# Values and output gates of a gated linear attention layer as seven half-size products through DRAM

## The chip, the core and the metric

The kernel runs on one NeuronCore of a Trainium2 chip. The metric is the device time of one execution in microseconds, median of the runs. Names of engines: PE is TensorE (matmul; PEld its weight loads), DVE VectorE, ACT ScalarE, POOL GpSimd, SP SyncE, whose queue issues the DMAs. Every engine executes its own instructions in the order in which the program holds them.

## The reference

A decoder trunk of two layers on x of 1 x 1024 x 1024 (sequence S, width D), all float32. Layer 0 mixes tokens with a dilated sliding-window attention, layer 1 with gated linear attention (GLA); each mixer is followed by an MLP with squared ReLU, each sub-layer has a norm ahead and a residual add behind. The change concerns the GLA mixer:

```python
proj = h @ w_in                       # 1024 -> 512 q, 512 k, 1024 v, 1024 g_out, 16 gate_lr
gk = gate_lr @ w_gate_up + b_gate
log_a = log_sigmoid(gk) / 16          # per head (4), chunks of 64 tokens
b = cumsum(log_a, axis=chunk)
q_t, k_t = q * DK**-0.5 * exp(b), k * exp(-b)
A = where(causal, q_t @ k_t.T, 0)
U = (k * exp(b_last - b)).T @ v       # per chunk; the state S runs over the chunks
o = A @ v + q_t @ S_prev              # 256 values per head
o = rmsnorm(o, norm_w) * silu(g_out)
out = o @ w_out
```

## The kernel before

**Arithmetic.** A float32 operand is cut in two parts of type fp32r: hi, rounded by ACT, and lo, the rest, subtracted on DVE (or POOL). A product is three matmuls: hi x hi, hi x lo, lo x hi (`mm3`, L212 to L215). Matmuls are 128 x 128 by 128 x 512; a block of 128 x 512 results over K = 1024 has 24 of them, in one of eight PSUM banks (`bank`).

**Seven products.** Larger products are cut into halves in each dimension and made as seven products of half size in place of eight, with sums of operands on DVE ahead (`sum1` to `sum4` on the left, differences of weights on the right) and sums of results behind. Class `Values` does this for the values of layer 0: 14 steps for each of three weight matrices, step n being half m of product q (`place`). In a step, `sums` copies finished accumulators out of PSUM (ACT) or adds them to such a copy (DVE), `prep(n + 2)` makes the two parts `dh` and `dl` of the weights of the step after next, `load(n + 5)` asks for weights, `product(n)` issues 24 matmuls. The accumulators are two sets of four banks, A and B, used in turns. `Halves` norms, transposes (`turn`) and cuts (`cut`) the left operand. The MLP (`Up`, `Down`) works in the same way.

**Order.** The program's order is written by hand (manual schedule); tiles come from pools: h8 (12 tiles of 8 KB a partition), k4 (25 of 4 KB), t2 (8 of 2 KB), and an instruction that needs a new tile waits until its last user is done. Work beside the matmuls is cut into steps: `tick()`, called twice per block, runs what `later(n, fn)` has set for that tick, then one entry of `steps`, then `W.pump()`, which loads and splits the next weights of class `Weights`; one of two is split on DVE, the other with `W.second` (POOL by default).

**From the MLP of layer 0 into GLA.** The last steps of `Down` are n = 52 and 53 and then `run_end` with four blocks t = 0 to 3. `first_rows` at n = 46 and 49 norms the first half of the rows; `norm_T` at n = 53 and in `run_end` transposes them into `hT` (eight h8 tiles, hi and lo); `norm_after` does the second half a few ticks later.

**GLA.** Heads go in two pairs. For pair 0: `values` (L292) makes V, 8 blocks of 128 tokens by 512, copied by ACT at L295; then the low-rank product for `lrT` (L1846, L1849) over both halves of the tokens; `start_gates(0)`; `gla_out_gates` (L1727) makes the output gates G, 8 blocks, each with the chain

```python
            act.activation(d, ps, AF.Exp, scale=-1.0)
            dve.tensor_scalar(d, d, 1.0, 3e38, op0=OP.add, op1=OP.min)
            act.activation(e, d, AF.Ln)
            act.activation(e, e, AF.Exp, scale=-1.0)
            dve.tensor_tensor(d, d, e, op=OP.mult)
            dve.scalar_tensor_tensor(e, d, 2.0, e, op0=OP.subtract, op1=OP.mult)
            dve.scalar_tensor_tensor(e, ps, -1.0, e, op0=OP.mult, op1=OP.mult)
```

(L1734 to L1740) and a multiplication by the norm weight on POOL (L1741). Then `gla_keys(h)` (L1799) makes queries and keys of a head: four times half a product (`dense_T`), with `gates` (L1747: bias product pg, Abs, Exp, Ln on ACT, a scan on DVE, subtractions on POOL) started half a head ahead. `gla_unit(h)` (L1648) puts the head's attention into `steps`: `a_step` (scores, masked into AM at L1658), `u_step` (state), `o_step` (output, norm factor `rstd_of`, gate). So the unit of head h runs in the ticks of later products: head 0's in the keys of head 1, head 1's in those of head 2 and the first blocks of the second `values`, head 2's in the keys of head 3, head 3's in the output projection. Order of the products: V pair 0, low rank, G pair 0, keys 0, 1, 2, V pair 1, G pair 1, keys 3.

Of the kernel before, what the change touches and what calls it, by code (L numbers as in the profile page):

```python
# [9 lines left out]
F32 = mybir.dt.float32  # L10
# [4 lines left out]
OP = mybir.AluOpType  # L15
# [26 lines left out]
def hybrid_trunk(ctx, tc, x, norm_mix, norm_mlp, norm_fin, a_in, a_out, g_in, g_up, g_b, g_nw,  # L42
# [68 lines left out]
    class Weights:  # L111
        def __init__(self):
            self.slots = []
            self.ndma = 0
            self.nprep = 0
            self.used = 0
            self.freed = 0
            self.limit = 5
            self.second = pool
            self.parts = {}  # L120
            self.raws = {}

        def add(self, src):
            self.slots.append(src)

# [8 lines left out]
        def prep(self, eng=pool):  # L134
# [12 lines left out]
            act.activation(hi, src, AF.Copy)  # L147
            eng.tensor_tensor(lo, src, hi.bitcast(F32), op=OP.subtract)  # L148
# [26 lines left out]
    def add_wide(w, c0):  # L175
        for j in range(4):
            W.add(cols(w, c0, 512, 2 * j, 2))

# [4 lines left out]
    def add_rows(w, k0):  # L183
        for k in range(2):
            W.add(w[P * (k0 + k):P * (k0 + k + 1), :])
# [3 lines left out]
    def plan_gla():  # L189
        for pair in range(2):  # L190
            if pair == 1:
                add_two(g_in, 512 + DK * 2, DK * 2)
            add_wide(g_in, 1024 + 512 * pair)
            if pair == 0:
                W.add(cols(g_in, 3072, RANK))
            add_wide(g_in, 2048 + 512 * pair)
            for h in ((0, 1), (3,))[pair]:
                add_two(g_in, 512 + DK * h, DK * h)
        for k in range(0, KT, 2):
            add_rows(g_out, k)  # L200
# [45 lines left out]
    def new_hT():  # L246
        return ([h8([P, 2, S], F32R, "hTh") for _ in range(4)],
                [h8([P, 2, S], F32R, "hTl") for _ in range(4)])

# [16 lines left out]
    def norm_T(xn, pair, hT):  # L266
        for kp in range(4):
            norm_T1(xn, pair, kp, hT)

    def norm_T1(xn, pair, kp, hT):  # L270
        transpose_pair(lambda k, i: xn[i][:, 256 * kp + 128 * k:256 * kp + 128 * k + 128],
                       hT[0][kp][:, :, 256 * pair:256 * pair + 256],
                       hT[1][kp][:, :, 256 * pair:256 * pair + 256])

    def mov(hT, kt, half):
        return tuple(t[kt // 2][:, kt % 2, 512 * half:512 * half + 512] for t in hT)

    def stat(hT, kt, lo, step=1):
        return tuple(t[kt // 2][:, kt % 2, lo:lo + (P - 1) * step + 1:step] for t in hT)

    def dense_T(w, hT, half, done):

        ps = bank("pd")
        for kt in range(KT):
            a, b = mov(hT, kt, half)
# [6 lines left out]
    def values(blocks):  # L292
        w = W.take(4)
        V = [h8([P, 4, 512], F32, "V") for _ in range(2)]
        dense_wide(w, hT, blocks, lambda n, ps: act.activation(V[n // 4][:, n % 4, :], ps, AF.Copy), True)  # L295
        return V

    def dense_wide(w, hT, blocks, done, last=False):
        for n, (lo, step) in enumerate(blocks):
            ps = bank("pd")  # L300
            for kt in range(KT):
                a, b = stat(hT, kt, lo, step)
                wh, wl = w[kt // 2]
                mm3(ps, a, b, wh[:, kt % 2, :], wl[:, kt % 2, :], kt == 0, kt == KT - 1)
                if last and n == len(blocks) - 1 and kt % 2:
                    W.free(1)
                if kt == 3:
                    tick()
            done(n, ps)
            tick()  # L310
# [27 lines left out]
    class Halves:  # L338

        def __init__(self, xs, wbc, up, spill=True):  # L340
# [10 lines left out]
        def norm(self, p, step=512):  # L351
            self.xn[p] = norm_scale([self.xs[p][:, 0, :], self.xs[p][:, 1, :]], self.wbc, step, self.y.pop(p, None))
            if self.spill:
                sp.dma_start(xmid[256 * p:256 * p + 256, :].rearrange("(i p) d -> p i d", p=P), self.xs[p])
# [29 lines left out]
        def cut(self, name, c):  # L384
# [4 lines left out]
                   "s3": a.get((1, 0)), "s4": a.get((0, 1))}[name]  # L389
            self.split(name, src, c, self.one, self.two if name in ("s2", "s3", "s4") else self.one)  # L390

        def sum3(self):
            a = self.a
            for c in range(2):
                self.combine(c, a[1, 0], a[0, 0], a[1, 0], OP.subtract)
# [49 lines left out]
        def finish(self):  # L445
# [40 lines left out]
            split("s3", a[1, 0], self.two)  # L486
# [248 lines left out]
    vscr = drp.tile([S, NG, AW], F32, name="vscr")  # L735

    class Values:

        STEPS = 14 * NG
        BLOCKS = ((1, 0), (0, 0), (0, 1), (1, 1), (1, 1), None, (1, 0))  # L740
# [9 lines left out]
        def load(self, n):  # L750
# [10 lines left out]
            sp.dma_start(t, cols(a_in, g * 3 * AW + 2 * AW + 512 * c, 512, 4 * k + 2 * m, 2))  # L761
# [57 lines left out]
        def copy(self, name, s, t):  # L819
# [9 lines left out]
        def add(self, name, s, t, g):  # L829
# [3 lines left out]
            row = 512 * half + 128 * t  # L833
            sp.dma_start(vscr[row:row + 128, g, 512 * quad:512 * quad + 512], c)

        def sums(self, n):
# [5 lines left out]
            for t in (2 * m, 2 * m + 1):  # L842
                if q == 1:
                    self.copy("c11", "B", t)
                elif q == 2:
                    self.add("c11", "A", t, g)
                elif q == 3:
                    self.copy("c22", "B", t)
                elif q == 4:
                    self.copy("c12", "A", t)  # L850
                elif q == 5:
                    self.add("c12", "B", t, g)
                elif q == 6:
                    self.copy("c21", "A", t)
                    self.add("c22", "A", t, g)

        def step(self, n):
# [3 lines left out]
            self.product(n)  # L861

# [347 lines left out]
    hs = Halves(x0, wbc, vals, False)  # L1210
# [163 lines left out]
    def out_proj(layer, wbc_row, o, up):  # L1374
# [5 lines left out]
        W.second = pool if layer else dve  # L1380
# [30 lines left out]
        W.second = pool  # L1411
# [3 lines left out]
        st = Halves(xs, wbc, up)  # L1415
# [14 lines left out]
    class Down:  # L1430
# [117 lines left out]
        def store_rows(self, p):  # L1548
            sp.dma_start(self.spill[256 * p:256 * p + 256, :].rearrange("(i p) d -> p i d", p=P), self.xs[p])

        def first_rows(self, p):
            self.xn = getattr(self, "xn", {})
            self.xn[p] = norm_scale([self.rows(2 * p), self.rows(2 * p + 1)], self.wbc)
            self.store_rows(p)

        def hook(self, n):
            if n == 40:
                self.wbc = load_norm_w(self.next_norm)
            if self.spill is not None:
                if n in (46, 49):  # L1560
                    self.first_rows(n // 49)
                elif n == 53:
                    plan_gla()
                    self.hT = new_hT()
                    norm_T(self.xn.pop(0), 0, self.hT)
# [6 lines left out]
            elif n >= 52:  # L1572
                for t in (2 * (n - 52), 2 * (n - 52) + 1):
                    self.fin[t] = (sm([P, 2], "ss"), k4([P, D], F32, "fin"))
                    self.half_out(t, 1)

# [8 lines left out]
        def run_end(self):  # L1585

            for t in range(4):
                if t == 1 and self.spill is not None:
                    norm_T(self.xn.pop(1), 1, self.hT)
# [3 lines left out]
                if self.spill is not None:  # L1593
                    if t % 2:
                        norm_after(self.xs, 2 + t // 2, self.wbc, self.hT, 4 + t // 2, self.spill)
                    tick()
# [17 lines left out]
    def norm_after(xs, pair, wbc, hT, lag, spill):  # L1614
        xn = norm_scale([xs[pair][:, 0, :], xs[pair][:, 1, :]], wbc)
        sp.dma_start(spill[256 * pair:256 * pair + 256, :].rearrange("(i p) d -> p i d", p=P), xs[pair])
        later(lag, lambda: norm_T(xn, pair, hT))

    def mlp(i, up, next_norm, spill):
# [5 lines left out]
        return d.hT if spill is not None else None  # L1625
# [3 lines left out]
    hT = mlp(0, up, norm_mix[1], xscr)  # L1629


    gc = r6([P, 1412], "gc")
# [283 lines left out]
```

## Time and profile before

| | |
|---|---|
| median of 3 runs | 2700.9 us (2699.88 to 2704.93) |
| the profiled execution's own time | 2703.08 us |
| its span, first to last instruction | 2701.3 us, mean granted clock 0.991 |
| busy PE / DVE / ACT / POOL | 2642.5 / 1788.8 / 1239.4 / 92.2 us |
| POOL instructions | 72 |
| DMA | 402.16 MB, mean 149 GB/s |

How to read profile rows: in a timeline, start and duration in us, engine, line, operation, result<-operands, shape, count, and in brackets the engine's idle time before it with what ended it. In windows, each stretch with its length, busy time of the engines with the number of instructions, the granted TensorE clock (1.00 is full) and DMA. Matmuls overlap in the pipeline: their pace is read from start to start, not from their durations.

### The profile page before, as it was taken

The numbers are of one execution on the slowest core, as the hardware profiler recorded it, in microseconds if no ns is written. First come the engines' busy times: TensorE is split into PE (matmuls) and PEld (weight loads), VectorE is DVE, ScalarE is ACT, GpSimd is POOL, SyncE is SP. The second block draws the span as 40 slices with busy tenths as digits, with TensorE's granted clock in tenths as the row PEclk, the third lists the DMA queues.
The fourth block names the chain that finished last, engine by engine and source line by source line (L and its number), as shares of the span: only waits on it lengthen the run. The fifth ranks groups of instructions, "written<-read, shape, count | busy, mean of one in ns | idle before, by whom it ended". The sixth has DMA issues, their size and how long they took to land.

```text
span 2701.3 us, 33223 instructions
## 1 busy us (share of the span) xinstructions
PE 2642.5 (98%) x12248; PEld 2184.9 (81%) x12248; DVE 1788.8 (66%) x2944; ACT 1239.4 (46%) x2300; POOL 92.2 (3%) x72
## 2 busy tenths in 40 slices
PE   7999999999999899999999999999999999999998
PEld 5888888888888787888888887778888788888887
DVE  7645788888888668666656672562557766656567
ACT  6332455555555345545533343432425555453343
POOL 0000000000000000000000001321200000000000
PEclk9999999999999999999999999999999999999999
DMA  4543455665657533444765453012223444486543
GB/s 152 171 149 113 106 155 137 155 156 140 157 145 206 170 117 123 158 166 138 288 234 187 144 170 113 24 36 66 74 98 114 148 163 139 151 315 217 189 148 125
DMA packets 311411, 402.16 MB, mean 149 GB/s; under 512 B 18864, under 2 KB 183216, under 8 KB 311248
## 3 DMA queue, kind: packets, MB, share of 16 engines
q1 hardware_dynamic: 311248, 400.04, 46.7%
q8 instruction: 96, 1.57, 0.2%
q14 instruction: 67, 0.55, 0.1%
HBM read 267.13 MB, written 107.68 MB: 139 GB/s over the span
## 4 chain that ended last, share of the span: by engine, by line
PE 59%; DVE 5%; ACT 2%; issue 1%; DVEq 0%; ACTq 0%
PE pB L1503 13%; PE pA L1503 10%; PE pX L629 8%; PE pd L213 5%; PE pd L215 5%; PE pd L214 5%; PE pV L629 5%; PE pZ L629 2%; PE pY L629 2%; PE pT L263 1%; PE pO L1678 1%; PE pU L1664 0%; PE pO L1677 0%; PE pT L366 0%; DVE wbl L567 0%
## 5 line engine op out<-in xcount | busy, mean ns | idle before, releaser
L1503 PE MATMUL pB<-dh 128*128 128x512 f32 x512 | 199.4, 389 | 0.0
L1503 PE MATMUL pB<-dh,dl 128*128 128x512 f32 x512 | 199.2, 389 | 0.0
L1503 PE MATMUL pB<-dl,dh 128*128 128x512 f32 x512 | 199.2, 389 | 0.0
L222 DVE TENSOR_TENSOR dl<-sin,dh 128x1024 fp32r<-128x1024 f32 x112 | 136.6, 1220 | 42.9 <-ACT dh L219 42.3
L629 PE MATMUL pV<-s4h,wd 128*128 128x512 f32 x448 | 153.6, 405 | 6.3 <-DVE rb L654 6.3
L219 ACT ACTIVATE dh<-sin 128x1024 fp32r<-128x1024 f32 x112 | 117.8, 1052 | 88.4 <-PE pB L1503 35.5
L924 ACT ACTIVATE pt<-pt,orow 128x128 f32<-128x128 f32 (+1 forms) x192 | 85.0, 444 | 148.0 <-DVE orow L922 143.5
L219 ACT ACTIVATE dh<-kept 128x1024 fp32r<-128x1024 f32 x64 | 67.9, 1061 | 183.3 <-DVE kept L1468 136.5
L1503 PE MATMUL pA<-dh 128*128 128x512 f32 x384 | 149.4, 389 | 0.0
L1503 PE MATMUL pA<-dl,dh 128*128 128x512 f32 x384 | 149.4, 389 | 0.0
L1503 PE MATMUL pA<-dh,dl 128*128 128x512 f32 x384 | 149.4, 389 | 0.0
L567 DVE TENSOR_TENSOR wbl<-t,wbh 128x1024 fp32r<-128x1024 f32 x56 | 68.6, 1225 | 73.6 <-ACT wbh L566 73.6
L1503 PEld LDWEIGHTS pB<-dh,dl 128*128 128x128 f32 x512 | 96.1, 188 | 20.0
L1503 PEld LDWEIGHTS pB<-dl,dh 128*128 128x128 f32 x512 | 96.1, 188 | 19.9
L1503 PEld LDWEIGHTS pB<-dh 128*128 128x128 f32 x512 | 96.1, 188 | 19.8
L567 DVE TENSOR_TENSOR wal<-raw,wah 128x512 fp32r<-128x512 f32 x112 | 76.2, 687 | 47.7 <-ACT wah L566 47.7
L629 PEld LDWEIGHTS pV<-s4h,wd 128*128 128x128 f32 x448 | 85.7, 191 | 25.8 <-DVE rb L654 8.0
L638 ACT ACTIVATE c<-c 128x512 f32<-128x512 f32 x64 | 40.4, 632 | 134.6 <-DVE c L666 83.2
L213 PE MATMUL pd<-whi,hTh 128*128 128x512 f32 x256 | 100.5, 393 | 0.0
L148 POOL TENSOR_TENSOR wlo<-raw,whi 128x1024 fp32r<-128x1024 f32 x16 | 40.0, 2499 | 1765.9 <-ACT whi L147 1762.9
L215 PE MATMUL pd<-whi,hTl 128*128 128x512 f32 x256 | 99.7, 389 | 0.0
L214 PE MATMUL pd<-wlo,hTh 128*128 128x512 f32 x256 | 99.6, 389 | 0.0
(307 smaller groups left out, 7458.0 us busy)
## 6 DMA issues: line engine op xcount, KB each, us to landing
sin<-acts SPq DMA_DIRECT2D x112, 512.0 KB, 3.7
raw<-in_mlp_w_up_dram SPq DMA_DIRECT2D x64, 512.0 KB, 5.7
acts<-s SPq DMA_DIRECT2D x64, 512.0 KB, 3.4
raw<-in_mlp_w_down_dram SPq DMA_DIRECT2D x64, 512.0 KB, 4.6
raw<-in_attn_w_in_dram SPq DMA_DIRECT2D x96, 256.0 KB, 4.4
cw<-c SPq DMA_DIRECT2D x192, 128.0 KB, 2.3
acts<-c SPq DMA_DIRECT2D x64, 256.0 KB, 2.1
kept<-in_mlp_w_down_dram SPq DMA_DIRECT2D x32, 512.0 KB, 5.0
```

What stands on the lines that cost most here:

```text
L148: eng.tensor_tensor(lo, src, hi.bitcast(F32), op=OP.subtract)
L213: pe.matmul(ps, sh, mh, start=start, stop=False)
L214: pe.matmul(ps, sh, ml, start=False, stop=False)
L215: pe.matmul(ps, sl, mh, start=False, stop=stop)
L219: act.activation(hi, src, AF.Copy)
L222: dve.tensor_tensor(lo, src, hi.bitcast(F32), op=OP.subtract)
L263: pe.transpose(ps[:, k, 128 * i:128 * i + 128], src(k, i), ident)
L567: self.remain(lambda: dve.tensor_tensor(lo, src, hi.bitcast(F32), op=OP.subtract))
L629: pe.matmul(st[b], u[:, k, :], v, start=first and k + n == 0, stop=k == 3 and n == 2, skip_group_check=True)
L638: act.activation(r, r, AF.Relu)
L924: act.activation(pt[:, i, :128 * n], pt[:, i, :128 * n], AF.Exp, scale=-1.0, bias=m, accum_out=self.row[:, r, HD:HD + 1])
L1503: pe.matmul(self.acc[s][t], a[:, k, c], b[:, k, :], start=fresh and m + k + v == 0, stop=m == 7 and k == 1 and v == 2, skip_group_check=True)
```

## The change

Values and output gates of all four heads are made first, as 2 x 14 steps of a new class `Mixed(Values)`: first the gates (g = 0, weight columns from 2048), then the values (g = 1, from 1024). Results go to DRAM (`ggscr`, `gvscr`), from where `load_head` reads 1 MB each of V and G per head, three ticks into that head's keys. The four quarters of the gates stay in h8 tiles (`gq`); `gate()`, called after each product from step 7 on, closes one piece (128 x 512) and opens the next, one piece per step. The left operand is cut by `Halves` for seven products; a11, a12, a22 and a21 (cut in steps 20 and 21) then serve as `hT` for the keys. `between` spreads the norms and cuts over `run_end`; `turn(0)` and `turn(1)` stand in steps 52 and 53.

The order afterwards is: gates, values, low rank, keys 0, 1, 2, 3, and each head's unit runs in the keys of the next. `start_gates(0)` follows the first half of the low-rank product. Outputs are treated in pairs of blocks (one bank, one `rstd_of` for two). The norm weight of GLA is multiplied into the rows of the output weights (`add_rows(..., by)`). All work of POOL in GLA (subtractions in `gates`, one of the q_s products, second weight splits) goes to DVE; POOL keeps memsets.

```diff
+    class Mixed(Values):
+        STEPS = 28
+        def source(self, g):
+            return g_in, (2048, 1024)[g]
+        def copy(self, name, s, t, g):
+            if g:
+                return super().copy(name, s, t, g)
+            if t == 0:
+                self.quad[name] = h8([P, 4, 512], F32, "gq")
+            c = self.c[name, t] = self.quad[name][:, t, :]
+            act.activation(c, self.acc[s][t], AF.Copy)
+        def made(self, c, g, rows, cols):
+            if g:
+                sp.dma_start(gvscr[rows, cols], c)
+            else:
+                self.todo.append((c, rows, cols))
+        def gate(self):
+            if self.open is not None:
+                c, rows, cols, d, e = self.open
+                dve.tensor_tensor(d, d, e, op=OP.mult)
+                dve.scalar_tensor_tensor(e, d, 2.0, e, op0=OP.subtract, op1=OP.mult)
+                dve.scalar_tensor_tensor(c, c, -1.0, e, op0=OP.mult, op1=OP.mult)
+                sp.dma_start(ggscr[rows, cols], c)
+                self.open = None
+            if self.todo:
...
+                act.activation(d, c, AF.Exp, scale=-1.0)
+                dve.tensor_scalar(d, d, 1.0, 3e38, op0=OP.add, op1=OP.min)
+                act.activation(e, d, AF.Ln)
+                act.activation(e, e, AF.Exp, scale=-1.0)
+                self.open = c, rows, cols, d, e
...
+    def gla_values():
+        hs, m = down.hs, down.mixed
+        m.product(0)
+        hs.turn(2)
+        m.prep(3)
+        m.load(4)
+        m.product(1, [0, 1])
+        hs.turn(3)
+        m.product(1, [2, 3])
...
+        for n in range(4, m.STEPS):
+            m.sums(n)
+            if n == 4:
+                hs.cut("s2", 1)
+            m.prep(n + 2)
+            m.load(n + (4 if n < 5 else 5))
+            if n == 4:
+                m.load(9)
+            m.product(n)
+            if n == 4:
+                hs.sum4()
+                hs.cut("s4", 0)
+            elif n == 5:
+                hs.cut("s4", 1)
+                hs.sum3()
+                hs.cut("s3", 0)
+            elif n == 6:
+                hs.cut("s3", 1)
+                hs.cut("a22", 0)
+            elif n == 7:
+                hs.cut("a22", 1)
+            if n >= 7:
+                m.gate()
+            if n == 22:
+                plan_gla()
+                W.limit = 3
+            if n in (20, 21):
+                hs.cut("a21", n - 20)
+            if n >= 24:
+                W.pump()
+        for t in range(4):
+            m.add("c21", "B", t, 1)
...
+        def between(self, t):
+            hs, mixed = self.hs, self.mixed
+            if t == 0:
+                mixed.rounded(0)
+                hs.cut("a12", 0)
+                mixed.remain(0)
+            elif t == 1:
+                hs.rstd(2)
+                hs.cut("a12", 1)
+                mixed.prep(1)
+            elif t == 2:
+                hs.norm(2)
+                hs.cut("a11", 0)
+            else:
+                hs.rstd(3)
+                hs.cut("a11", 1)
+                hs.norm(3)
+                mixed.prep(2)
...
-            pool.tensor_tensor(m, m, a, op=OP.subtract)
+            dve.tensor_tensor(m, m, a, op=OP.subtract)
...
-    V = values(nat)
+    hT = gla_values()
     W.take(1)
...
         act.activation(lrT[:2 * RANK, 512 * half:512 * half + 512], ps[:2 * RANK, :], AF.Copy)
+        if half == 0:
+            start_gates(0)
         tick()
     W.free(1)
-    start_gates(0)
-    G = gla_out_gates()
     W.limit = 4
-    for h in range(2):
-        gla_unit(h, V, G, *gla_keys(h))
-    keys = gla_keys(2)
...
+    for h in range(GH):
+        rows = []
+        later(3, lambda: rows.extend((load_head(gvscr, h, "V"), load_head(ggscr, h, "gG"))))
+        got = gla_keys(h)
+        gla_unit(h, *rows, *got)
```

More of the change, by code (lines that the diff above doesn't have):

```diff
@@ L290, in dense_T @@
         tick()
[L292 to L310, printed above, removed]
     class Split:
@@ L843, in sums @@
                 if q == 1:
-                    self.copy("c11", "B", t)
+                    self.copy("c11", "B", t, g)
                 elif q == 2:
@@ L1559, in hook @@
             if self.spill is not None:
[L1560 to L1565, printed above, removed]
+                if n == 46:
+                    self.mixed = Mixed()
+                    self.hs = Halves(self.xs, self.wbc, self.mixed, self.spill)
+                    self.hs.norm(0)
+                elif n == 49:
+                    self.hs.norm(1)
+                elif n >= 52:
+                    self.hs.turn(n - 52)
+                    for k in range(2):
+                        self.mixed.load(2 * (n - 52) + k)
             elif 44 <= n < 48:
@@ L1844, in hybrid_trunk @@
         for kt in range(KT):
-            for n, t in enumerate(mov(hT, kt, half)):
+            for n, t in enumerate(hT[half][kt // 4].parts(kt % 4)):
                 pe.matmul(ps[:2 * RANK, :], W.both[:, kt, :], t, start=kt + n == 0, stop=kt + n == KT)
```

225 lines of the change are left out of this document (105 added, 120 removed).

## The prediction

> **What bounds the kernel now.** I read the page first: the share of each engine and the chain of work that ended last.
>
> ```profile
> PE 2642.5 (98%) x12248; PEld 2184.9 (81%) x12248; DVE 1788.8 (66%) x2944; ACT 1239.4 (46%) x2300; POOL 92.2 (3%) x72
> ...
> PE 59%; DVE 5%; ACT 2%; issue 1%; DVEq 0%; ACTq 0%
> ```
>
> PE is busy 98% of the span and holds the chain, so a matmul that goes is worth its full time wherever PE waits for nobody. Next I cut the stage that changes into stretches: the first values product, the keys of head 0, the keys of head 2, and the second values and gates.
>
> ```profile
> 1623.80:1671.10 47.30, 47.30 (x227) 39.53 (x226) 12.89 (x24) 12.59 (x23) 2.62 (x2) 1.00 0.35 107
> 1723.30:1752.50 29.20, 27.15 (x110) 20.33 (x109) 16.18 (x24) 12.42 (x25) 14.48 (x11) 0.94 0.05 20
> 1788.30:1826.00 37.70, 35.85 (x157) 28.40 (x157) 23.63 (x69) 16.22 (x51) 8.61 (x9) 0.95 0.15 50
> 1826.00:1916.80 90.80, 90.80 (x402) 74.99 (x400) 30.54 (x62) 29.02 (x52) 16.23 (x11) 1.00 0.18 60
> ```
>
> Columns: stretch, length, then busy time of PE, PEld, DVE, ACT and POOL, granted clock, DMA. In the dense products (first and last row) PE is never idle and the clock is 1.00, while DVE works a third of the time or less. PE loses time only in the keys: 2.05 us idle in one stretch, 1.85 us in the other, each with a lower clock.
>
> ```profile
> 1660.30 0.60 ACT L295 ACTIVATE V<-pd 128x512 f32<-128x512 f32 x1 [4.84 <-PE pd L215]
> ```
>
> ACT copies a finished block and then waits 4.84 us for PE: one block of 24 matmuls takes 0.60 + 4.84 = 5.44 us, 0.227 us a matmul. Values and output gates of both halves are 32 blocks, 174.1 us.
>
> **What goes: matmuls.** Seven products of half size for each of the two matrices are 28 steps of 24 matmuls, 672 for 768: 96 x 0.227 = 21.8 us less PE work, all of it on the path. Other matmuls and transposes keep their number.
>
> **What goes: GpSimd's stalls.**
>
> ```profile
> 1734.84 0.66 PE L1821 MATMUL pk<-ident,kdT 128*128 128x128 f32 x4 [2.05 <-DVE kdT L1816]
> ...
> 1736.01 0.63 PE L215 MATMUL pd<-hTh,wlo 128*128 128x512 f32 x1
> 1736.43 0.63 PE L213 MATMUL pd<-hTh,whi 128*128 128x512 f32 x1
> ...
> 1732.06 2.39 DVE L1815 TENSOR_TENSOR kdT<-k_m,dec 128x256 f32<-128x256 f32 x1
> 1734.38 0.41 DVE L1816 TENSOR_TENSOR kdT<-pd,es 128x256 f32<-128x256 f32 x1
> ```
>
> PE waited 2.05 us for kdT because DVE's L1815, running beside a GpSimd instruction, took 2.39 us where the next one of the same size took 0.41 us. Afterwards matmuls start every 0.42 us, not 0.227: half clock. With a clock of 0.94 over 29.2 us that costs 1.75 us more, and 0.95 over 37.7 us costs 1.9 us in the other stretch. With GpSimd silent both stalls should go: 2.05 + 1.75 + 1.85 + 1.9 = 7.6 us. If DVE's longer queue keeps either, the bound is 0.
>
> On the half clock the Trainium skill speaks otherwise (TensorE: Matmul & The Clock Gate, HAM oscillation — how this bites in real kernels): it puts the limit for idle gaps at about 3.4 us. Here a gap of about 2 us was enough, so I price stalls with the half clock; by the page's rule the two half-clock terms that I add further down, 3.3 us, would fall away.
>
> **What is added: the gates' chain.** In the order of the changed program's instructions, step n (n from 7) holds on DVE: sums of finished quarters, the weight's difference (in 8 of 14 steps), the low part dl for step n+2, the three closing operations of the gate before, and the opening one (TS) of this gate. On ACT: copies of finished quarters, dh for step n+2, then Exp, Ln, Exp of this gate. Both run in order, so this is a ring: Ln waits for TS; the next step's copies and dh wait behind Ln and Exp; dl waits for dh; the three closings and the next TS wait behind dl. Its links, from the gates of before and the values of layer 0:
>
> ```profile
> 1685.94 0.43 DVE L1735 TENSOR_SCALAR gd<-gd 128x512 f32<-128x512 f32 x1 [4.84 <-ACT gd L1734]
> 1687.73 0.69 DVE L1738 TENSOR_TENSOR gd<-gd,ge 128x512 f32<-128x512 f32 x1 [1.36 <-ACT ge L1737]
> 1688.46 0.69 DVE L1739 SCALAR_TENSOR_TENSOR ge<-gd,ge 128x512 f32<-128x512 f32 x1
> 1689.19 0.69 DVE L1740 SCALAR_TENSOR_TENSOR ge<-pd,ge 128x512 f32<-128x512 f32 x1
> 1689.80 1.21 DVE L1769 TENSOR_TENSOR_SCAN ga<-gc,gmn 128x512 f32<-128x512 f32 x1
> ...
> 1686.41 0.63 ACT L1736 ACTIVATE ge<-gd 128x512 f32<-128x512 f32 x1 [0.49 <-DVE gd L1735]
> 1687.07 0.63 ACT L1737 ACTIVATE ge<-ge 128x512 f32<-128x512 f32 x1
> ...
> 67.42 1.07 ACT L826 ACTIVATE c<-pB 128x512 f32<-128x512 f32 x2
> 68.38 1.06 ACT L795 ACTIVATE dh<-raw 128x1024 fp32r<-128x1024 f32 x1
> ...
> 80.42 1.06 ACT L795 ACTIVATE dh<-kept 128x1024 fp32r<-128x1024 f32 x1 [1.35 <-DVE kept L771]
> ...
> 79.17 1.22 DVE L771 TENSOR_TENSOR kept<-kept 128x1024 f32<-128x1024 f32 x1
> 81.51 1.22 DVE L801 TENSOR_TENSOR dl<-kept,dh 128x1024 fp32r<-128x1024 f32 x1 [1.13 <-ACT dh L795]
> 82.66 1.22 DVE L771 TENSOR_TENSOR kept<-kept 128x1024 f32<-128x1024 f32 x1
> ```
>
> From start to start: TS to Ln 0.47, Ln to Exp 0.66, Exp 0.63, two copies 0.96 (67.42 to 68.38), dh to dl 1.09 (80.42 to 81.51), dl 1.15, three closings 2.07 (1687.73 to 1689.80). A step with copies takes 7.03 us round the ring. With a difference and two sums instead (0.43 + 1.15, two sums priced as one 1024-wide operation, difference to dh 1.25) it is 7.14 us; without either 6.07, and 6.2 with four sums. In steps 20 and 21 ACT also rounds a21, 1.0 us more for the next ring. Gates are open from step 7 to 22. The 15 rings between come to 7 x 7.03 + 2 x 8.03 + 4 x 7.14 + 6.2 + 6.07 = 106.1 us, where PE's 15 steps need 81.6. DVE's own work there, 15 x (1.15 + 2.07 + 0.43) + 19 x 1.15 for differences, sums and a21 = 77 us, would fit; the order does not let it.
>
> PE cannot run ahead of the ring: product n (even) writes its third block into a bank that step n-1 must first have copied or summed, so of two steps' lead it keeps little. The next late thing after the ring starts is therefore always a bank.
>
> **Where the ring starts.** The second turn now stands before run_end's products, so these run unbroken up to 1623.8, the same moment as before; the first of their four blocks ends at 1623.8 - 3 x 2.72 = 1615.6 and DVE can add it at 1616.1. From there DVE has no pause worth the name.
>
> ```profile
> 1619.80 1.06 ACT L243 ACTIVATE junk<-xs 128x1024 bf16<-128x1024 f32 x1 [2.10 <-DVE xs L1509]
> ...
> 1623.09 2.74 DVE L256 SCALAR_TENSOR_TENSOR xn<-xs,y,wbc 128x512 f32<-128x512 f32 x4
> ```
>
> A norm's factor takes 3.3 us from its second Square to the scaling (1619.80 to 1623.09), the scaling 2.74. During run_end DVE has four adds (half of 1.15 each, 2.3), four low parts of a12 and a11 (4.6), three dl (3.45), two factors (6.6) and two scalings (5.5): 22.5, to 1638.6. Then 23 operations or pairs of 1.15 (one dl, sums 1 to 4, parts of s1, s2, s4, s3 and a22, two sums of quarters, two dl: 26.5), four weight differences with their dl at 82.66 - 79.17 = 3.49 (14.0), and waits for ACT at s1 and the last dl, estimated at 2.5 from the 1.13 us wait above: 43.0, to 1681.6, the first TS. On the way PE waits some 2.5 us for xn of the last rows, as DVE is at 1636 with them where PE wants them at 1634; it costs nothing more, for the ring decides later.
>
> **The end of the stage.** The last TS is at 1681.6 + 106.1 = 1787.7. PE's product 24 gets its third bank 2.3 us later (Ln, Exp and one copy), does 18 matmuls (4.1) and three steps (16.3), and pays about 1.5 for half clock: 1811.9. The quarter c21 finds no free buffer until the store of c11 has landed: 0.6. So 1812.5 - 1623.8 = 188.7 us. Before, the same work took 174.1 plus two turns of 1.8 (47.3 less 8 x 5.44 = 3.8 for both): 177.9. The stage gets longer by 10.8 us although 21.8 us of matmuls are gone.
>
> **The low-rank product.** It used to be followed by 8 blocks of gates; now its bias product pg comes straight after each half.
>
> ```profile
> 1678.58 0.59 ACT L1849 ACTIVATE lrT<-pd 32x512 f32<-32x512 f32 x1 [3.12 <-PE pd L1846]
> 1679.63 0.69 ACT L1762 ACTIVATE ga<-pg,gc 128x512 f32<-128x512 f32 x1 [0.46 <-PE pg L1761]
> ...
> 1691.04 0.73 ACT L1757 ACTIVATE eb<-ga 128x256 f32<-128x256 f32 x2 [3.34 <-DVE ga L1769]
> ```
>
> The first pg waits for its copy, 0.59 and two hand-overs, 1.0 us. The second waits for a copy that stands on ACT behind three Exp of half 0, which wait for DVE's scan: pg to Abs 0.7, three functions 2.0, subtraction 0.7 (now on DVE), scan 1.2, Exp 1.1, copy 0.6 make 6.3 from the first pg, where 16 matmuls take 3.6: 2.5 us, and 1.8 at half clock after it. Together 5.3 us; the bounds are 1.0 (no half clock, copy early) and 7.
>
> **Hidden or nothing.** Heads read values and gates back in 1 MB loads, asked for three ticks into one head and needed in the next.
>
> ```profile
> ol<-oscr SPq DMA_DIRECT2D x2, 1024.0 KB, 9.7
> ```
>
> A load of that size landed in 9.7 us; the shortest time to its first use, in head 0, is four more half blocks and a tick, over 15 us. If two loads shared the rate, about 4 us would show, once. DVE in the heads gets GpSimd's subtractions, the q_s product and half of the weight parts, but only four normalising chains instead of eight: nothing, at worst the rival below. W.second changes nothing in layer 0, where the trace has no POOL work.
>
> **Sum.** +10.8 + 5.3 - 7.6 = +8.5 on a span of 2701.3: 2709.8. The profiled execution took 2703.08, its span lies 0.4 above the median of the runs, 2700.9; on the median I say 2709.
>
> **The rivals.**
> 1. PE keeps the stage: the ring does not hold it, because the lead of two steps or faster hand-overs hide it. Then 28 steps at 5.44, no half clock but for 4.3 us at the late rows: -21.8 - 7.6 + 5.3 + 4.3 = -19.8, 2681. For it: DVE's 77 us of work in 81.6, and PE at 47.30 of 47.30 in the old stage. Against it: the links above, each in order. It decides when a ring is under 5.44 us. Chance 0.13.
> 2. The ring is there but shorter, say 6.2 us each, as some links overlap: 13 us less, 2696. Chance 0.12.
> 3. DVE becomes the bound in the heads too: with GpSimd's five operations in its order and waits for Ln, a half head takes more than PE's 17 us (half of 37.7 less the 3.7 lost); 1.5 us for each of six halves, 2718. Against it: in 1788.30:1826.00 DVE was busy 23.63 of 37.70. Chance 0.08.
> 4. Buffers: SP, in order, waits for a free k4 tile before a load, and stores queue behind it; 8 us more, 2717. Chance 0.07.
>
> My forecast has 0.60, with its own range of 2701 to 2717 (5.3 and 7.6 between their bounds, 3 us on the start). All rivals but the first lie within 2690 to 2721, which leaves out about 0.17. A measurement of this kernel tells 0.2%, 5.4 us, from no change. Faster by more: rival 1 and a third of rival 2, 0.17. Within: the rest of rival 2 and the lower part of my own range, 0.25. Slower: 0.58.
>
> **What would show it.** In the changed profile: PE waits at every second product of the new stage for a copy or sum on ACT or DVE, some 1 to 3 us each; successive TS about 7 us apart; granted clock under 1.00 there; no POOL work and no 2 us wait at kdT; a wait of about 2.5 us at the second pg. Wrong would be: steps of 5.44 us between the gates, PE full in the new stage, or its loss elsewhere, in the heads or behind a load.

## The result and the profile after

The changed kernel takes 2721.7 us, median of four runs (2714.8 to 2722.0), where the kernel before took 2700.7 on the same chip: a ratio of 1.0068, 95% interval 1.0049 to 1.0088. It is slower, as forecast, by more than forecast: 2709 was said, and 2721.7 lies 0.7 us above the end of the range. The profiled execution took 2722.04 us with a span of 2719.9, 18.6 more than the span before.

The page of the changed kernel, engines and chain:

```profile
PE 2633.1 (97%) x12152; PEld 2168.6 (80%) x12152; DVE 1864.6 (69%) x2995; ACT 1269.5 (47%) x2320; POOL 1.8 (0%) x7
...
PE 53%; DVE 8%; ACT 4%; issue 2%; DMA 1%; SPq 0%; DVEq 0%; ACTq 0%
```

96 matmuls are gone (12152 for 12248), but PE's busy time fell by only 9.4 us instead of 21.8, in part because more of the rest runs at the lower clock (0.989 in the mean for 0.991), and the chain now goes through DVE (8% for 5%) and ACT (4% for 2%). The stretches show where (length, busy time of PE, PEld, DVE, ACT and POOL, granted clock, DMA): from the transposition of the last rows to the low-rank product; then the first keys; then heads 0, 1 and 2, each from its score block to that of the next head.

```profile
1632.30:1811.80 179.50, 158.35 (x652) 125.78 (x653) 134.24 (x177) 87.55 (x134) 0.95 (x1) 0.95 0.37 113
...
1824.20:1853.90 29.70, 29.70 (x121) 22.76 (x121) 17.05 (x32) 12.62 (x25) 0.00 (x0) 0.94 0.18 63
1853.90:1897.20 43.30, 40.75 (x170) 31.15 (x170) 25.76 (x67) 15.64 (x47) 0.00 (x0) 0.92 0.20 68
1897.20:1938.80 41.60, 39.03 (x169) 30.47 (x168) 25.03 (x65) 15.64 (x47) 0.00 (x0) 0.96 0.31 102
1938.80:1979.50 40.70, 37.08 (x182) 30.45 (x181) 24.39 (x57) 14.05 (x39) 0.00 (x0) 1.00 0.49 159
```

The new stage keeps PE idle for 21 us at a clock of 0.95, where the dense products before had neither. The heads lose time too, 2.6, 2.6 and 3.6 us of idle PE and clocks of 0.92 and 0.96 in the first two; that part the forecast did not have.

The new stage first. The opening operation (TS) of the gates on DVE, first two and last two of 16:

```profile
1678.45 0.42 DVE L872 TENSOR_SCALAR gd<-gd 128x512 f32<-128x512 f32 x1
1685.36 0.42 DVE L872 TENSOR_SCALAR gd<-gd 128x512 f32<-128x512 f32 x1
...
1775.65 0.42 DVE L872 TENSOR_SCALAR gd<-gd 128x512 f32<-128x512 f32 x1
1785.13 0.42 DVE L872 TENSOR_SCALAR gd<-gd 128x512 f32<-128x512 f32 x1
```

Fifteen rings (from one TS to the next) take 1785.13 - 1678.45 = 106.7 us, where 106.1 was forecast; the first is 6.91 us long, the last 9.48. PE's waits in that stretch and at the bias product after it, from PE's timeline:

```profile
1687.64 0.50 PE L783 MATMUL pA<-dh,s3h 128*128 128x512 f32 x1 [1.72 <-ACT gq L850]
...
1717.10 0.80 PE L783 MATMUL pB<-dh,a12h 128*128 128x512 f32 x1 [3.49 <-DVE gq L798]
...
1771.04 0.80 PE L783 MATMUL pB<-dh,s4h 128*128 128x512 f32 x1 [3.71 <-ACT c L793]
...
1787.41 0.50 PE L783 MATMUL pA<-dh,s3h 128*128 128x512 f32 x1 [2.77 <-ACT c L793]
...
1816.37 1.12 PE L1827 MATMUL pg<-lrT,gc 32*128 32x512 f32 x2 [0.68 <-ACT lrT L1917]
...
1823.17 1.12 PE L1827 MATMUL pg<-lrT,gc 32*128 32x512 f32 x2 [1.88 <-ACT lrT L1917]
...
1825.49 0.63 PE L213 MATMUL pd<-a11h,wlo 128*128 128x512 f32 x1
1825.92 0.63 PE L211 MATMUL pd<-a11h,whi 128*128 128x512 f32 x1
```

In the new stage's waits shown here it is a bank each time, freed late by a copy on ACT or a sum on DVE. The stage ends at 1811.8 (forecast 1812.5, but from a run_end that ended at 1623.8; in this trace it ends 2.1 us earlier, at 1621.7). Behind the second bias product matmuls start every 0.43 us: half clock.

Now the heads, at the end of head 0. PE's output matmuls (two to a line), then ACT, then DVE at the same time:

```profile
1886.38 0.59 PE L1758 MATMUL pO<-Sb,q_s 128*128 128x256 f32 x2
1886.81 0.59 PE L1759 MATMUL pO<-V,AM 128*128 128x256 f32 x2
1889.03 0.70 PE L1758 MATMUL pO<-Sb,q_s 128*128 128x256 f32 x2 [1.62 <-ACT gy L1760]
1889.56 0.59 PE L1759 MATMUL pO<-V,AM 128*128 128x256 f32 x2
```

```profile
1888.17 0.20 ACT L228 ACTIVATE t<-v 128x2 f32<-128x2 f32 x1 [4.23 <-DVE v L227]
1888.40 0.20 ACT L229 ACTIVATE y<-t 128x2 f32<-128x2 f32 x1
1888.52 0.37 ACT L1760 ACTIVATE gy<-pO 128x256 f32<-128x256 f32 x1
```

```profile
1887.64 0.42 DVE L1894 SCALAR_TENSOR_TENSOR q_s<-pd,es 128x256 f32<-128x256 f32 x1
1887.98 0.16 DVE L227 TENSOR_SCALAR v<-gss 128x2 f32<-128x2 f32 x1
```

Two output blocks now share one bank (`po[:, i, :]`). Before PE may write the second, ACT must have read the first (the Square, L1760). ACT was idle for 4.23 us, but in its order the norm factor of the pair before stands ahead (L228, L229), which waits for DVE's L227, which stands behind the q_s operations. So PE waits 1.62 us for an instruction that needs nothing but PE's own result.

### The profile page after: what moved, and what is told of

Same layout as the page of the kernel before. It is cut to its first block, busy times and chain, and to the rows that moved or that the text cites. A ratio compares the mean times of both kernels' runs of the same rounds, so it can differ in the third digit from the quotient of the medians.

```text
span 2719.9 us, 33059 instructions
## 1 busy us (share of the span) xinstructions
PE 2633.1 (97%) x12152; PEld 2168.6 (80%) x12152; DVE 1864.6 (69%) x2995; ACT 1269.5 (47%) x2320; POOL 1.8 (0%) x7
## 4 chain that ended last, share of the span: by engine, by line
PE 53%; DVE 8%; ACT 4%; issue 2%; DMA 1%; SPq 0%; DVEq 0%; ACTq 0%
PE pB L1515 12%; PE pA L1515 10%; PE pX L589 8%; PE pV L589 5%; PE pd L211 3%; PE pd L212 3%; PE pd L213 3%; PE pZ L589 2%; PE pY L589 2%; PE pB L783 1%; DVE dl L768 1%; PE pA L783 1%; PE pT L325 1%; ACT dh L762 1%; PE pO L1758 0%
## 5 line engine op out<-in xcount | busy, mean ns | idle before, releaser
L220 DVE TENSOR_TENSOR dl<-kept,dh 128x1024 fp32r<-128x1024 f32 x64 | 78.4, 1225 | 24.9 <-ACT dh L217 19.0
L589 PE MATMUL pX<-s2h,wbh 128*128 128x512 f32 x224 | 90.2, 403 | 4.4 <-ACT wbh L526 3.9
L589 PE MATMUL pX<-s3h,wgh 128*128 128x512 f32 x224 | 91.4, 408 | 1.0 <-ACT e L594 0.9
L768 DVE TENSOR_TENSOR dl<-kept,dh 128x1024 fp32r<-128x1024 f32 x40 | 48.6, 1224 | 63.4 <-ACT dh L762 63.4
```

Of the source, the lines that this page charges most:

```text
L220: dve.tensor_tensor(lo, src, hi.bitcast(F32), op=OP.subtract)
L589: pe.matmul(st[b], u[:, k, :], v, start=first and k + n == 0, stop=k == 3 and n == 2, skip_group_check=True)
L768: dve.tensor_tensor(lo, t, hi.bitcast(F32), op=OP.subtract)
```

## The experiments

The kernel before ran beside each of them. Its median moved between 2700.7 and 2702.4 us, so ratios are compared, each with its 95% interval.

| kernel | us | ratio to the kernel before |
|---|---|---|
| changed kernel | 2721.7 | 1.0068 (1.0049 to 1.0088) |
| the same again | 2720.1 | 1.0061 (1.0045 to 1.0077) |
| unpair | 2710.5 | 1.0029 (1.0020 to 1.0038) |
| ring | 2704.0 | 1.0006 (0.9995 to 1.0016) |
| ringdiff | 2694.0 | 0.9970 (0.9959 to 0.9982) |
| ringahead | 2693.8 | 0.9973 (0.9964 to 0.9982) |
| nogate | 2691.0 | 0.9953 (0.9936 to 0.9970) |
| pg | 2716.1 | 1.0058 (1.0044 to 1.0072) |
| poolback | 2723.7 | 1.0076 (1.0059 to 1.0093) |
| secondpool | 2717.5 | 1.0061 (1.0048 to 1.0075) |
| before_dve | 2700.9 | 0.9993 (0.9984 to 1.0003) |
| all | 2680.5 | 0.9927 (0.9913 to 0.9940) |
| all2 | 2676.1 | 0.9903 (0.9888 to 0.9918) |

**unpair: a bank for each output block.**

```diff
-                st["o"] = bank("pO").rearrange("p (i v) -> p i v", i=2), sm([P, 2], "gss"), ...
+                st["o"] = [], sm([P, 2], "gss"), t2([P, 2, DV], F32, "gy")
             po, ss, y = st["o"]
+            po.append(bank("pO")[:, :DV])
...             # matmuls, Square and scaling use po[i] for po[:, i, :]
```

> Edit: in the heads each output block gets a PSUM bank of its own again; the pair keeps its common square sums, norm factor and store. Theory A (the bank shared by two blocks is what the forecast missed): PE's second block waits for ACT's Square of the first because both lie in one tile; six waits of 7.9 us in all, and the half clock behind them. Three heads then lose 6.5, 4.5 and 3.2 us less: 2721.7 - 14 = 2708, and the time from the first score block of head 0 to that of head 3 shrinks from 125.5 to about 111 us. Theory B (the heads lose their time to DVE's longer queue or to the loads of values and gates): PE finds another wait at the same places, 2721, the three heads stay at 125 us.

Measured: 2710.5, ratio 1.0029. At the same place ACT's Square is as late as it was, but PE goes on:

```profile
1888.67 0.36 ACT L1761 ACTIVATE gy<-pO 128x256 f32<-128x256 f32 x1
```

```profile
1886.96 0.59 PE L1760 MATMUL pO<-V,AM 128*128 128x256 f32 x2
1887.39 0.60 PE L1759 MATMUL pO<-Sb,q_s 128*128 128x256 f32 x2
1887.83 0.59 PE L1760 MATMUL pO<-V,AM 128*128 128x256 f32 x2
```

The same three heads, in windows (columns as above):

```profile
1855.50:1892.30 36.80, 36.80 (x170) 29.43 (x169) 24.07 (x61) 15.13 (x45) 0.00 (x0) 1.00 0.24 81
1892.30:1929.00 36.70, 36.70 (x169) 29.35 (x168) 25.36 (x67) 15.54 (x47) 0.00 (x0) 1.00 0.35 115
1929.00:1966.90 37.90, 37.10 (x181) 30.34 (x180) 24.91 (x63) 14.27 (x41) 0.00 (x0) 1.00 0.51 156
```

111.4 us for 125.6, with DVE and ACT as busy as in the changed kernel: the shared bank it was, and not the loads. DVE's queue still makes the Square late, but with a bank of its own for each block that costs PE nothing. The Trainium skill (PSUM — Partial Sum Buffer, PSUM bank collisions raise a hardware error) says that two engines must not touch the same bank on the same partitions at once, even at different addresses, and that one guards by bank, not by address. The program guards in this way, and the trace agrees in that PE waited for a read of other columns of its bank, 1.62 us at the place shown; no run lets two engines collide.

**ring: two lines moved.**

```diff
                 c, rows, cols, d, e = self.open
+                act.activation(e, d, AF.Ln)
+                act.activation(e, e, AF.Exp, scale=-1.0)
                 dve.tensor_tensor(d, d, e, op=OP.mult)
...
                 dve.tensor_scalar(d, d, 1.0, 3e38, op0=OP.add, op1=OP.min)
-                act.activation(e, d, AF.Ln)
-                act.activation(e, e, AF.Exp, scale=-1.0)
                 self.open = c, rows, cols, d, e
```

> Edit: two lines moved: Ln and the second Exp of a gate are issued at the start of the next step's gate, behind that step's copies and rounding, instead of at the end of their own. Same instructions, same tiles. Theory A (the ring through ACT and DVE holds the new stage): what is left of the ring is TS, Ln, Exp, three closings, 3.9 us; DVE's own order then sets 5 to 7.4 us a step (difference, rounding, low part in steps with a difference), 94 us for the 15 steps that now take 106.6, and 2 us of half clock: 2721.7 - 14 = 2708. Theory B (DVE's amount of work, or buffers, hold the stage, not the order): 106 us again, 2720 or more.

**nogate: the stage without the gates' chain.**

```diff
-                self.todo.append((c, rows, cols))
+                sp.dma_start(ggscr[rows, cols], c)
```

> Leaves out: the activation of the output gates (Exp, the opening operation, Ln, Exp, the three closings) for all 16 blocks in the new stage; the raw sums are stored instead. Theory A (the gates' chain is what lengthens the stage): between step 7 and step 22 PE is full, a step is 5.44 us, and the stage falls from 188 to about 162 us: 2696. Theory B (the products' own sums, differences, roundings or loads hold PE anyway): less than 10 us come back, 2712 or more.

**ringdiff and ringahead: differences one step earlier, and the next weights' loads too.** ringdiff is ring with the first of these edits, ringahead has both.

```diff
+            if 7 <= n < m.STEPS - 3:
+                m.total(n + 3)
             m.product(n)
...
                 W.limit = 3
+                for _ in range(3):
+                    W.dma()
```

> Edit: the ring kernel (Ln and second Exp behind the next step's copies and rounding); besides, a weight's difference is formed one step earlier, so that its rounding on ACT never waits for it, and the first three loads of the following weights are issued at step 22 instead of 24. What the ring kernel still lost against the kernel without gates (163.2 against 149.7 us from the second turn to the low-rank product): theory A, the hand-overs difference, rounding, low part on DVE and a weight load of 2.3 us that DVE's low part waits for at 1787; DVE's own work is about 80 us in 15 steps, under PE's 81.6, so the stretch falls to 153 to 156 us and the time by 7 to 10 from the ring kernel's 2704: 2695. Theory B: DVE's amount of work holds the rest, 161 to 163 us, 2703.

> The ringahead kernel without its early weight loads (Ln and second Exp moved, differences one step earlier). It splits the 10 us between ring (2704) and ringahead (2694). If the weight load is what PE waited 3.68 us for at 1785, with half clock behind: 2698 to 2700, and that wait is there again. If the differences did it alone: 2694 to 2696, no wait over 2 us after 1720.

Measured: ring 2704.0, ringdiff 2694.0, ringahead 2693.8, nogate 2691.0. The stage from the last rows' transposition to the low-rank product, in the window of each kernel:

ring:

```profile
1637.40:1800.60 163.20, 152.22 (x653) 122.67 (x653) 134.41 (x177) 86.87 (x134) 0.95 (x1) 0.98 0.42 128
```

ringdiff:

```profile
1634.70:1787.40 152.70, 149.16 (x652) 122.24 (x653) 132.78 (x177) 87.22 (x134) 0.95 (x1) 0.99 0.45 139
```

nogate:

```profile
1635.80:1785.50 149.70, 147.31 (x653) 120.88 (x654) 97.01 (x113) 60.29 (x86) 0.96 (x1) 1.00 0.46 142
```

This settles the ring. The same instructions (177 on DVE, 134 on ACT) with the same busy time (134.2, 134.4 and 132.8 us on DVE) take 179.5, 163.2 and 152.7 us, by order alone; without any gate it is 149.7. DVE's amount of work, 133 us in 153, leaves 3 us of cost. The ring kernel gave 16.3 us in its stage and not 14, and ringdiff 10.5 more. The traces come to this stage up to 5 us apart (1632.3 to 1637.4); counted from the last product of run_end it takes 190.1, 173.8, 163.4 and, without gates, 160.4 us, with the same differences. In the six traces with the unchanged order (the changed kernel twice, unpair, pg, poolback, secondpool) it takes 189.7 to 190.3.

One guess fell. In the ring kernel PE waited 3.68 us behind a low part that waited for a weight load:

```profile
1787.48 1.22 DVE L153 TENSOR_TENSOR wlo<-raw,whi 128x1024 fp32r<-128x1024 f32 x1 [3.07 <-ACT whi L152]
```

ringdiff issues that load no earlier, its DVE waits as long (2.99 us, at 1774.5), and PE does not notice: with the differences out of the way DVE is ahead by then. The load was only late because the queue behind it was.

**pg: the bias product later, inside other matmuls.**

```diff
-        later(2, second)
-        later(3, third)
+        soon = h == half == 0
+        later(1 if soon else 2, second)
+        later(2 if soon else 3, third)
...
-        act.activation(lrT[:2 * RANK, 512 * half:512 * half + 512], ps[:2 * RANK, :], AF.Copy)
-        if half == 0:
-            start_gates(0)
+        if half:
+            dve.tensor_copy(lrT[:2 * RANK, 512:1024], ps[:2 * RANK, :])
+        else:
+            act.activation(lrT[:2 * RANK, 0:512], ps[:2 * RANK, :], AF.Copy)
+            later(2, lambda: start_gates(0))
...
-            start_gates(2 * h + half + 1)
+            if h or half:
+                start_gates(2 * h + half + 1)
+            else:
+                later(1, lambda: start_gates(1))
```

> Edit: the bias product of half 0 starts four tiles into half 1 of the low-rank product, that of half 1 after four tiles of the first keys; the copy of half 1 goes to DVE. Theory A (forecast): the waits of 0.68 and 1.88 us at the bias product, their hand-overs and the half clock after them go, 12.4 us from the low-rank product's start to the first keys become 9.6 or 10, and 2.3 us of half clock behind: 2721.7 - 5 = 2717. Theory B (the half clock falls elsewhere, since a clock once lowered returns by its own time): only the waits go, 2.8 us, 2719.

Measured: 2716.1, ratio 1.0058, whose interval overlaps that of the unedited kernel. The two waits are gone from the trace, and a new one of 1.75 us stands at kdT, up to 1832.9.

**poolback, secondpool and before_dve: what became of GpSimd's stalls.** poolback puts four operations for each half head back on POOL:

```diff
-            dve.tensor_tensor(m, m, a, op=OP.subtract)
+            pool.tensor_tensor(m, m, a, op=OP.subtract)
...             # likewise the two subtractions in second() and q_s[:, bl, CH:] in q_done
```

> Edit: the three subtractions of the gate preparation and one product of q_s go back to GpSimd, as in the kernel before; all else is the changed kernel. Theory A (DVE beside GpSimd is what cost 7.6 us in the heads before): the wait at kdT and the one at the output block come back, 2.05 and 1.85 us with half clock: up to 2729. Theory B (those stalls came from the queue on DVE at that place, not from GpSimd): 2721, no wait at kdT.

secondpool puts back the second low part of each pair of weights, in heads 0 to 2:

```diff
     W.limit = 4
+    W.second = pool
     for h in range(GH):
+        if h == GH - 1:
+            W.second = dve
```

> Edit: every second weight block's low part in heads 0 to 2 goes to GpSimd again, as in the kernel before (2.47 us each there); nothing else goes back. Theory A (this is the GpSimd work beside which DVE's 0.41 us operations took 2.39): DVE's two kdT operations become longer than 0.42 us on the mean, and the wait at kdT returns: up to 7.6 us, 2722 to 2729. Theory B (the stall was one of order, DVE's queue): means of 0.42 us stay, 2721.

before_dve does the opposite in the kernel before:

```diff
-            self.second = pool
+            self.second = dve
...             # and the other places that choose POOL for a weight's low part
```

> The kernel before, with every second weight block's low part on DVE instead of GpSimd (all other GpSimd work stays). Theory A (the forecast's 7.6 us belong to GpSimd's low parts of 2.47 us, beside which a DVE operation of 0.42 us waits for their end): the two waits of 2.05 and 1.85 us and their half clock go, 2701 - 7.6 = 2693 to 2697. Theory B (DVE's longer queue keeps the stalls: two low parts of 1.2 us now stand ahead of the keys' operations): 2699 to 2703, a wait for kdT or the output block is still there.

Measured: 2723.7, 2717.5 and 2700.9, ratios 1.0076, 1.0061 and 0.9993: none can be told from its unedited kernel. In poolback and in secondpool PE waits nowhere for kdT; each puts a part of GpSimd's work back, and no run puts back all of it. In the secondpool trace, DVE and then POOL:

```profile
1858.03 1.63 DVE L1881 TENSOR_TENSOR kdT<-k_m,dec 128x256 f32<-128x256 f32 x1
...
1877.03 0.42 DVE L1881 TENSOR_TENSOR kdT<-k_m,dec 128x256 f32<-128x256 f32 x1
```

```profile
1856.89 2.48 POOL L153 TENSOR_TENSOR wlo<-raw,whi 128x1024 fp32r<-128x1024 f32 x1 [26.29 <-ACT whi L152]
```

DVE's 0.42 us operation takes 1.63 us when it starts inside POOL's, and ends 0.3 us after POOL's end (1859.66 and 1859.37). The Trainium skill (SBUF — State Buffer, Who interferes with whom) states this: a DVE instruction with two SBUF inputs contends with a GpSimd instruction that reads SBUF, since its second input comes through a shared port, and that port is an exclusive lock. The trace agrees. But no wait of PE followed, for kdT was not late. And in before_dve, where low parts are made on DVE instead, the stalls stayed, and a new one came at 1925.4. PE there:

```profile
1734.25 1.12 PE L1821 MATMUL pk<-ident,kdT 128*128 128x128 f32 x4 [3.34 <-DVE kdT L1816]
...
1802.27 0.70 PE L1678 MATMUL pO<-V,AM 128*128 128x256 f32 x2 [1.55 <-DVE AM L1658]
...
1925.39 0.70 PE L1678 MATMUL pO<-V,AM 128*128 128x256 f32 x2 [2.16 <-DVE AM L1658]
```

and DVE ahead of the first of them:

```profile
1727.98 3.45 DVE L148 TENSOR_TENSOR wlo<-raw,whi 128x1024 fp32r<-128x1024 f32 x2
1731.35 0.74 DVE L1763 TENSOR_SCALAR gmn<-pg,gc 128x512 f32<-128x512 f32 x1
1732.01 0.68 DVE L1814 TENSOR_TENSOR k_m<-pd,eb 128x512 f32<-128x512 f32 x1
```

The keys' operations now stand on DVE behind two low parts of weights that come at the wrong time. In the kernel before, one of these was on POOL:

```profile
1731.81 2.36 POOL L148 TENSOR_TENSOR wlo<-raw,whi 128x1024 fp32r<-128x1024 f32 x1
```

There DVE's L1815 ended 0.28 us after it (1734.45 and 1734.17) and took 2.39 - 0.41 = 1.98 us too long, nearly the whole of PE's wait of 2.05. So the block by GpSimd was real; but where its work goes to DVE at the same place, that work delays the same operations from DVE's own queue. before_dve does not silence GpSimd (its other work stays, and L1815 still takes 1.07 us), so no run shows the old order with the low parts gone from both engines. In the changed kernel's order the low parts come early enough, and DVE waits for PE instead:

```profile
1827.32 2.36 DVE L153 TENSOR_TENSOR wlo<-raw,whi 128x1024 fp32r<-128x1024 f32 x2 [0.25 <-ACT whi L152]
1831.60 0.69 DVE L1880 TENSOR_TENSOR k_m<-pd,eb 128x512 f32<-128x512 f32 x1 [1.91 <-PE pd L213]
```


**all and all2: the edits together.** all is unpair, ringahead and pg; all2 gives head 0 one more tick before its first transposition of kdT:

```diff
-                later(2, kd_T)
+                later(2 + (h == half == 0), kd_T)
```

> Edit: the edits of unpair, ringahead and pg together. Theory A (three separate losses): unpair gave 11 to 14 us, the ring 16 to 18, differences and early loads 7 to 10 more, the bias product 3 to 5: 2721.7 - (37 to 47) = 2675 to 2685, faster than the kernel before by 0.6 to 0.9%. Theory B (they cover each other, for instance the weights become late): 2690 or more.

> The kernel all, with the first transposition of kdT in head 0 one tick later, since there PE waits 1.75 us for kdT, which stands on DVE behind two low parts of weights (2.36 us together). Theory A: wait and half clock behind it go, 2 to 4 us: 2677 to 2679. Theory B (the next wait takes its place, since PE is only let through to the same DVE operations): 2680 to 2681.

Measured: 2680.5 and 2676.1, ratios 0.9927 (0.9913 to 0.9940) and 0.9903 (0.9888 to 0.9918): faster than both kernels. The intervals of all and all2 overlap, so what the one tick is worth is not settled. The edits add up: ratios of 1.0065 (the mean of the two measurements) less 0.0036, 0.0092 and 0.0007 make 0.993. The wait that is gone in all2's trace, as it stands in that of all:

```profile
1804.38 0.66 PE L1893 MATMUL pk<-ident,kdT 128*128 128x128 f32 x4 [1.75 <-DVE kdT L1888]
```

**after_again: how far one measurement carries.**

> The changed kernel once more, unedited, since its first four runs spread from 2714.8 to 2722.0 us and the smaller experiments (bias product 2716, second weight part on GpSimd 2717, small GpSimd work 2724) are to be weighed against it. Theory A (its median is 2721 to 2722): the second weight part on GpSimd gains some 4 us and the bias product some 5. Theory B (most of the spread is half clock that falls differently from run to run, and the median is 2717 to 2719): the second weight part changes nothing that can be told, the bias product 1 to 3 us; the same waits of PE at the output block, 7.9 us, stand in its trace either way.

Measured: 2720.1 us (2711.5 to 2725.4), ratio 1.0061 (1.0045 to 1.0077), between the two theories; the waits at the output block stand there with 7.8 us. By the ratios secondpool's gain of some 4 us becomes none, and pg's lies between 1 and 3 us, which its interval does not tell from none.

## Why the prediction was right, and by how much it was not

**Matmuls and the ring: right, with its size.** Counted from the end of run_end (1621.7 in this trace, 1623.8 in the forecast), the first TS comes after 56.8 us for 57.8, fifteen rings take 106.7 for 106.1 and what follows the last TS 26.7 for 24.8: 190.1 us for 188.7, so +12.2 for +10.8. The sum is closer than its terms: single rings last 5.9 to 9.5 us, where 6.07 to 8.03 were forecast. PE's waits of over 1 us are seven in the stage, 1.6 to 3.7 us, where one at every second product, 1 to 3 us each, was forecast. That order and not work causes the loss is shown by ring, ringdiff and nogate. Rival 1 (PE keeps the stage) comes nearly true once the order is changed: in ringdiff the gates cost 3 us of the stage.

**The bias products: right in the trace.** Waits of 0.68 and 1.88 us, for which 1.0 and 2.5 were forecast with their hand-overs, and a clock of 0.94 over the next 29.7 us, 1.8 us as forecast: 4.6 for 5.3. That the half clock came was chance in part: in unpair's trace the same two waits stand and the clock behind them is 1.00. What removing them is worth is not settled, as in pg another wait took their place.

**GpSimd's stalls: gone as forecast, but GpSimd's silence is not enough for it.** No wait at kdT is left. But putting a part of GpSimd's work back does not bring the stall, and moving its low parts to DVE in the kernel before does not remove it. The step "with GpSimd silent both stalls should go" read the block rightly and left out where the work goes; the order on DVE around the keys decides, and the bound that the forecast gave for it ("if DVE's longer queue keeps either") was the better half of the sentence.

**Hidden or nothing: the step that failed.** "Only four normalising chains instead of eight: nothing" counted what the pairing saves on DVE and not what it ties together: two blocks in one bank. Six waits, 7.9 us, and half clock behind them are 14 us in the profiled execution (125.6 against 111.4 us) and 0.36% or about 10 us between the medians. In pg's trace the same waits stand without half clock, and the three heads take 120.8 us, 9.4 more than in unpair; the rest of the 14 is clock. Rival 3 put a loss in the heads too, by DVE as the bound; the price was near, the mechanism was another.

**The sum.** In the profiled executions the MLP's first product starts at 2088.5 for 2068.0, 20.5 later: 2.1 earlier ahead of the stage, 12.2 later in it and 10.4 behind it. Of the last 4.6 belong to the bias products (12.4 us from the low-rank product to the first keys, where PE's work in it took 9.6 before, and 1.8 of clock) and 14.2 to the bank, so 8.4 are left for the stalls that went, where 7.6 was forecast. That 8.4 is a rest, not measured apart, and holds more than the two stalls: in the output projection PE waited 1.83 us for wlo at 2018.0 before, with half clock behind, and 0.40 and 0.82 us without it after. Some 1.9 us come back in the MLP. The forecast's +8.5 lacked the bank.

## What to carry to other kernels

A chain that goes to and fro between two in-order engines costs its latency, not its work, as the stage here did: give it a place in each queue where its input is ready, by issuing its second half one step later, before counting how busy the engines are. When an edit merges small operations by putting two results into one PSUM bank, ask who reads the first while the second is written, and what stands ahead of that reader in its queue. And before counting a stall as gone because its neighbour in the trace falls silent, ask where the neighbour's work goes: in DVE's own queue it stood ahead of the same operations.

## What the runs showed of the hardware that was not expected

The same waits did not cost the same clock. Heads 0, 1 and 2 of the changed kernel have the same two waits, 2.6 to 3.6 us of idle PE in each, and clocks of 0.92, 0.96 and 1.00; in pg's trace the same six waits stand at 1.00 in all three. From 1630 us to the end of the heads, the changed kernel's trace has half clock only in stretches of 3.4 or 6.9 us, so one costs 1.7 or 3.4. They begin at 1634.3, 1716.2, 1770.9, 1787.9, 1825.5, 1890.3 and 1934.7, each a whole number of 3.41 us steps behind the one before (24, 16, 5, 11, 19, 13). The Trainium skill (TensorE: Matmul & The Clock Gate, Part 1: The HAM clock gate) describes a free-running window of about 3.4 us in which activity is counted, which would make the price of a wait a matter of where it falls. The trace agrees with steps of that length. By the limit on gaps that the same page gives (HAM oscillation — how this bites in real kernels) waits this short should be free. The trace does not agree with a limit of that size (0.92 in head 0, where the longest wait is 1.62 us), and no run here moves a wait within a step on purpose. So a half-clock term, right in one stretch, can be absent in the next; that this is also why the changed kernel's runs spread over 14 us was not tested.
